# The first load becomes 32 contiguous rows, and the last diagonal tile moves into the last batch

## The chip, the cores and the metric

The kernel runs on one core of a Trainium2 chip. The metric is the device time of one execution in microseconds (us); the time given is the median of several executions. A profile is taken of one execution by the hardware, and the views below are read from it.

## What is computed

The input x has 4 batches of 4224 x 4224 numbers in fp32, 285.47 MB. The reference, cut to what matters:

```python
ps = np.cumsum(np.cumsum(x, axis=1), axis=2)   # 2D prefix sums
diag = np.diagonal(ps, axis1=1, axis2=2)       # their diagonal
return np.cumsum(diag, axis=1)                 # and its running sum
```

The output is 4 x 4224 numbers. Diagonal element i is the sum of the square x[:i+1, :i+1], so element (r, c) of x adds to every diagonal element from max(r, c) on. It is enough to know, for every m, the sum of all elements with max(r, c) = m; two running sums over m then give the output.

## The kernel before

The 4224 rows and columns are cut into 11 groups of 384 (`NG`, `GW`). Rows are loaded in strips of 768 (`F2` = 6 rows in each of 128 partitions), by DMAs issued from GpSimd (POOL) that turn fp32 into bf16 on the way; three strip buffers are in use (`NBUF`), so a load waits in POOL's queue until the strip that held its buffer has been used up. All of these loads share one queue and are served in the order in which they are issued.

For each strip `add_up` (L374) splits the elements by whether the row or the column is the larger index. Columns to the right of the diagonal block are summed down the rows by TensorE, which multiplies them with a selecting column of ones (`columns`, L363) and adds them into a tile `d` of 11 x 384 in PSUM. The diagonal block is split with a mask on VectorE (L387, L388). What lies below the diagonal is summed along the rows, partly on ScalarE (`act_sum`, L264), partly on VectorE (`row_sums`, L271). After the strips of a batch two scans on VectorE (L520) make the running sums.

The last batch ends with the last group of rows, 3840 to 4223 (`T0` = 3840, `TB` = 4096), and is ordered by hand so that little work is left after the last byte. Its rows are taken in two parts. Part a is the 256 rows from 3840 to 4095, held as `part_a` (two rows per partition, 128 apart). Part b is the last 128 rows, held as `part_b` in four blocks of `R` = 32 rows; each row of a block is spread over four partitions (`k` = 4), so a block is 128 partitions of a quarter row.

- The head (L66 to L69): before anything else, the SyncE queue (SP) loads the last 528 columns of part a in fp32, 256 pieces of 2112 bytes. It is summed by L97, its diagonal parts are masked at L322 to L325, and the result `ahead` is kept until the end.
- The tile of part b on the diagonal, 128 x 128 (`diag_b`, L427), is loaded by POOL after the first strip of the last batch and used after its second strip (L428 to L435), where all the sums that are known so far are weighed into `fin_a` and `fin_b`, the rows of the last group's outputs (`weigh_b`, `weigh_rows`, on TensorE).
- After the last whole strips POOL loads the remaining columns of part a in two cuts, 1536 to 3696 and 0 to 1536 (L472 to L474), and the four blocks of part b with their first 4096 columns (L475 to L490), the last block in two pieces of 768 and 256 columns.
- The cuts of part a are folded to 256 columns by TensorE (`fold_in`, L255, into `fold_a`) and summed by ScalarE (L539, `asum`). Block 0 is weighed by eight matmuls with `weights4_h` (L537), copied (`by`, L542) and added. Blocks 1 to 3 are summed along the rows, each partly by ScalarE and partly by VectorE (`pair_sum`, L276), and weighed into `fin_b` and `fin_e` (L550 to L578). The output rows are `yl` (first 256, then up to the last 32) and `ye` (the last 32).

The order on each engine is the order of the program (`manual_schedule`, L62), and waits between engines are set from the use of the tiles. In the tail VectorE's queue therefore holds, in this order: a pair sum of block 1, the addition L554 that needs `fin_a`, a pair sum of block 2, two of block 3, and the addition L579. ScalarE's holds the two sums of `fold_a`, the copy `by`, one sum each of blocks 1, 2 and 3, and the copy L573.

Of the kernel before, what the change touches and what calls it, by code (L numbers as in the profile page):

```python
# [8 lines left out]
FP32 = mybir.dt.float32  # L9
BF16 = mybir.dt.bfloat16  # L10
I32 = mybir.dt.int32
AX = mybir.AxisListType
# [5 lines left out]
def kernel(  # L18
# [14 lines left out]
    nc = tc.nc  # L33

    B, H, W = x.shape
    N = H
    P = 128
    F = 3
    F2 = 2 * F
    GW = P * F  # L40
    NG = N // GW
    LB = B - 1
    LG = NG - 1
    T0 = LG * GW
    TB = N - P
# [3 lines left out]
    consts = ctx.enter_context(tc.tile_pool(name="consts", bufs=1))  # L49
# [4 lines left out]
    last = ctx.enter_context(tc.tile_pool(name="last", bufs=1))  # L54
# [3 lines left out]
    psum_s = ctx.enter_context(  # L58
        tc.tile_pool(name="psum_s", bufs=1, space=bass.MemoryType.PSUM)
    )  # L60
# [2 lines left out]

    HC = 528  # L66
    src_a = x[LB, T0:TB, :].rearrange("(h p) w -> p h w", p=P)
    head = last.tile([P, 2, HC], FP32, name="head")
    nc.sync.dma_start(out=head, in_=src_a[:, :, N - HC : N])  # L69

    def strip_tile():
        return strips.tile([P, F2, N], BF16, name="strip")
# [20 lines left out]
    prefetch()  # L93


    hs = last.tile([P, 3], FP32, name="hs")
    nc.vector.reduce_sum(out=hs[:, 0:2], in_=head, axis=AX.X)  # L97

    sel = consts.tile([P, 2 * NG - 1], BF16, name="sel")
    nc.vector.memset(sel, 0.0)  # L100
# [21 lines left out]
    for i in range(1, NBUF):  # L122
        prefetch()
    um3 = upper_mask(F)
    um1 = consts.tile([P, GW], BF16, name="um1")
    nc.vector.memset(um1, 1.0)
    nc.gpsimd.affine_select(
        out=um1,
        in_=um1,
# [10 lines left out]
        out=ident,  # L140
        in_=ident,
# [10 lines left out]
    ones_row = consts.tile([NG, GW], FP32, name="ones_row")  # L152
# [21 lines left out]
    def between_groups(name, turned):  # L174
# [25 lines left out]
    weights = counted("weights", P, GW, [(0, GW, 1, 1, -1)])  # L200
    nc.gpsimd.affine_select(
        out=weights,
        in_=weights,
# [5 lines left out]
    )  # L209


    R = P // 4
    steps = consts.tile([P, P], I32, name="steps")
    nc.gpsimd.iota(steps, pattern=[[4, P]], base=7, channel_multiplier=-1)
    nc.vector.tensor_single_scalar(
        out=steps, in_=steps, scalar=2, op=ALU.arith_shift_right
    )
    weights4 = consts.tile([P, P], FP32, name="weights4")
# [5 lines left out]
    def matmul(o, lhsT, rhs, start=False):  # L224
        nc.tensor.matmul(  # L225
            o, lhsT=lhsT, rhs=rhs, start=start, stop=False, skip_group_check=True
        )
# [19 lines left out]
            )  # L247
        )

    weights4_h = consts.tile([P, P], BF16, name="weights4_h")  # L250
    nc.vector.tensor_copy(out=weights4_h, in_=weights4)
    ones_col = consts.tile([P, 1], FP32, name="ones_col")
    nc.vector.memset(ones_col, 1.0)

    def fold_in(o, src, c0, c1, w, start=False):  # L255

# [7 lines left out]
    def act_sum(acc, src):  # L264
        w = src.shape[-1]
        dump = dumpool.tile([P, 2176], BF16, name="dump")
        nc.scalar.activation(  # L267
            out=dump[:, :w], in_=src, func=ACT.Copy, accum_out=acc
        )

    def row_sums(acc, src):  # L271
        nc.vector.reduce_sum(out=acc, in_=src, axis=AX.X)  # L272
# [3 lines left out]
    def pair_sum(acc, src):  # L276

        w = src.shape[-1] // 2
        if not pairs:
            pairs.append(last.tile([P, 288], FP32, name="pair"))  # L280
        pair = pairs[0]
        nc.vector.scalar_tensor_tensor(
            out=pair[:, :w],
            in0=src[:, :w],
            scalar=1.0,
            in1=src[:, w:],
            op0=ALU.mult,
            op1=ALU.add,
            accum_out=acc,
        )  # L290

    def masked(o, i, m, acc):
        nc.vector.scalar_tensor_tensor(  # L293
            out=o,
            in0=i,
            scalar=1.0,
            in1=m,
            op0=ALU.mult,
            op1=ALU.mult,
            accum_out=acc,  # L300
        )
# [12 lines left out]
        nc.vector.memset(rows3[i], 0.0)  # L314


    ahead = last.tile([P, 2], FP32, name="ahead")
    asum = last.tile([P, 2], FP32, name="asum")
    dtot = last.tile([P, 1], FP32, name="dtot")
    hu = last.tile([P, 3], FP32, name="hu")  # L320
    hmu = last.tile([P, 3, GW], BF16, name="hmu")
    for h in range(2):  # L322
        w = GW - h * P
        masked(hmu[:, h, :w], head[:, h, HC - w : HC], um1[:, :w], hu[:, h : h + 1])
    nc.vector.tensor_sub(out=ahead, in0=hs[:, 0:2], in1=hu[:, 0:2])  # L325

    whole_sums = last.tile([NG, LB, GW], FP32, name="whole_sums")
    last_sums = last.tile([NG, GW], FP32, name="last_sums")

    M0 = 2 * P  # L330
    E0 = GW - R

    for b in range(B):
# [18 lines left out]
        def weigh_b(rows, w, r0=0, start=False):  # L352

            matmul(fin_b[:, r0:], rows, w[..., : P - r0], start=start)

        def weigh_rows(rows, start=False):

            matmul(fin_a, rows[:, 0:1], weights[:, :M0], start=start)
            matmul(fin_a[:, P:], rows[:, 1:2], weights[:, :P])
            weigh_b(rows[:, 0:1], weights[:, M0:])  # L360
            weigh_b(rows[:, 1:2], weights[:, P:])
# [55 lines left out]
        for s in range(ns):  # L417
            strip = prefetched.pop(0) if prefetched else None
            if strip is None:
                strip = strip_tile()  # L420
                load_rows(strip, b, s * F2 * P)
            add_up(
                strip, F2, s * F2 * P, acc6[:, s], um6, by_rows=whole and s > 0
            )
            if not whole and s == 0:
                diag_b = last.tile([P, P], BF16, name="diag_b")
                nc.gpsimd.dma_start(out=diag_b, in_=x[b, TB:N, TB:N])  # L427
            if not whole and s == 1:  # L428
                row_sums(hs[:, 2:3], diag_b)
                masked(hmu[:, 2, :P], diag_b, um1[:, :P], hu[:, 2:3])  # L430
                nc.vector.tensor_sub(out=dtot, in0=hs[:, 2:3], in1=hu[:, 2:3])
                for h in range(3):
                    columns(LG, h * P, GW, hmu[:, h, : GW - h * P], h > 0)
                weigh_b(dtot, weights, start=True)
                weigh_rows(ahead, start=True)  # L435
        a6 = acc6[:, :ns]
        sum_up(a6)
        for h in range(2):
            ps = slice(h * HP, (h + 1) * HP)
            k = row_of(h)  # L440
            nc.vector.tensor_copy(  # L441
                out=r6[ps, k : k + 2 * ns : 2, :], in_=a6[ps, :, :, 1]
            )

        strip = strip_tile()
# [21 lines left out]
        if not whole:  # L467

            strip = strip_tile()
            part_a = strip[:, 0:2]  # L470
            part_b = strip[:, 2, :TB].rearrange("p (s c) -> p s c", s=4)
            acuts = [(1536, N - HC), (0, 1536)]  # L472
            for c0, c1 in acuts:
                nc.gpsimd.dma_start(out=part_a[:, :, c0:c1], in_=src_a[:, :, c0:c1])  # L474
            CB = TB // 4  # L475
            bcut = 768
            for sb, c0, c1 in (
                (0, 0, CB),
                (1, 0, CB),
                (2, 0, CB),  # L480
                (3, 0, bcut),
                (3, bcut, CB),
            ):
                r0 = TB + sb * R
                nc.gpsimd.dma_start(  # L485
                    out=part_b[:, sb, c0:c1],
                    in_=x[b, r0 : r0 + R, :TB].rearrange("r (k c) -> r k c", k=4)[
                        :, :, c0:c1
                    ],
                )  # L490

            fold_a = psum_s.tile([P, 2, 256], FP32, name="fold_a")
            c0, c1 = acuts[0]
            fcuts = [c0, c0 + 768, c0 + 2048, c1]
# [13 lines left out]
        c1 = mup.tile([NG, GW], FP32, name="c1")  # L508
# [10 lines left out]
        for i, (to, src) in enumerate(((c1, d), (c2, c1))):  # L519
            nc.vector.tensor_tensor_scan(  # L520
                out=to,
# [11 lines left out]
        ye = last.tile([1, R], FP32, name="ye")  # L533
        c0, c1 = acuts[1]
        fold_in(fold_a, part_a, c0, c1, 256)
        by_ps = psum_s.tile([P, P], FP32, name="fold")
        for c in range(0, CB, P):  # L537
            matmul(by_ps, part_b[:, 0, c : c + P], weights4_h, start=c == 0)
        for h in range(2):  # L539
            act_sum(asum[:, h : h + 1], fold_a[:, h])  # L540
        by = last.tile([P, P], FP32, name="by")
        nc.scalar.copy(out=by, in_=by_ps)  # L542
        weigh_b(ones_col[0:1], last_sums[0:1, M0:])
        weigh_rows(asum)
        weigh_b(ones_col, by)


        bsum = last.tile([P, 2, 2], FP32, name="bsum")
        esum = last.tile([P, 3], FP32, name="esum")
        act_sum(bsum[:, 0, 0:1], part_b[:, 1, :512])  # L550
        pair_sum(bsum[:, 0, 1:2], part_b[:, 1, 512:])
        for i in (1, 0):
            weigh_b(bsum[:, 0, i : i + 1], weights4, R)
        nc.vector.tensor_add(out=yl[:, :M0], in0=fin_a, in1=last_sums[0:1, :M0])  # L554
# [1 line left out]
            out=out[b, T0 : T0 + M0].unsqueeze(0), in_=yl[:, :M0]  # L556
        )
        nc.sync.dma_start(
            out=out[:LB, :].rearrange("b (g i) -> g b i", i=GW), in_=whole_sums
        )  # L560
        nc.sync.dma_start(
            out=out[b, :T0].rearrange("(g i) -> g i", i=GW), in_=last_sums[1:NG]
        )
        act_sum(bsum[:, 1, 0:1], part_b[:, 2, :448])
        pair_sum(bsum[:, 1, 1:2], part_b[:, 2, 448:])
        for i in (1, 0):
            weigh_b(bsum[:, 1, i : i + 1], weights4, 2 * R)


        act_sum(esum[:, 0:1], part_b[:, 3, :320])  # L570
        pair_sum(esum[:, 1:2], part_b[:, 3, 320:bcut])
        pair_sum(esum[:, 2:3], part_b[:, 3, bcut:])
        nc.scalar.copy(out=yl[:, M0:], in_=fin_b)  # L573
        nc.sync.dma_start(
            out=out[b, T0 + M0 : T0 + E0].unsqueeze(0), in_=yl[:, M0:E0]
# [35 lines left out]
```

## Time and profile before

| | before |
|---|---|
| median of 4 executions | 667.45 us (667.18 to 667.63) |
| the profiled execution | 667.42 us |
| its span, first to last instruction | 665.7 us |
| mean granted TensorE clock | 0.656 |
| TensorE busy | 206.5 us (31%) |
| VectorE busy | 380.2 us (57%) |
| ScalarE busy | 136.9 us (21%) |
| POOL busy | 31.7 us (5%) |
| pieces that the DMA queues moved | 7666, of which under 512 bytes 698, under 2 KB another 300 |
| head, SP: size, issue to landing | 528 KB, 4.0 us |
| `diag_b`, POOL: size, issue to landing | 32 KB (as bf16), 53.2 us |

Engines are PE (TensorE matmul), PEld (its weight loads), DVE (VectorE), ACT (ScalarE), POOL (GpSimd) and SP (SyncE). "L272" is line 272 of the kernel. A row of a timeline gives the start, the duration, the engine, line and operation, what is written and read with its shape, and in brackets how long the engine had been idle before it and what ended that. The digits of a row such as DMA are the busy share in 40 equal slices of the span, in tenths. The sizes of loads that turn fp32 into bf16 are counted as they are written. A long time from issue to landing means that a transfer stood in the queue behind others.

### The profile page before, as it was taken

The page shows a single profiled execution, that of the slowest core. Times are in us where ns is not written, and L with a number is a line of the kernel's source. Part 1 is how long each engine was busy: PE and PEld are TensorE (multiplying, and loading weights), DVE is VectorE, ACT ScalarE, POOL GpSimd, SP SyncE. Part 2 cuts the span into 40 slices and gives each one's busy share as a digit, 9 for nine tenths or more (in the row PEclk, how much of TensorE's full clock was granted, in tenths as well). Part 3 has the DMA queues.
Part 4 walks back from the last instruction along what each step waited for, and adds up shares of the span by engine and source line. Part 5 has one row for each costly group of instructions (what it writes and reads, how often), then busy time and mean ns, then how long its engine had stood idle before and what let it go on. Part 6 is the DMA issues. An engine that isn't in the chain of part 4 may idle for free.

```text
span 665.7 us, 2519 instructions
## 1 busy us (share of the span) xinstructions
PE 206.5 (31%) x956; PEld 94.7 (14%) x956; DVE 380.2 (57%) x174; ACT 136.9 (21%) x223; POOL 31.7 (5%) x60
## 2 busy tenths in 40 slices
PE   0070622303117143130311623503021354350427
PEld 0030211101003021010000311201000121220203
DVE  4160928476946173756794526456589433352866
ACT  0000121406300103040630020304063002030434
POOL 4300000000000000000000000000000000001000
PEclk9995857655558585665555957567565585765759
DMA  9999999999999999999999999999999999999998
GB/s 203 218 219 219 219 218 215 212 213 218 219 218 218 219 220 217 215 216 216 213 219 220 214 218 219 219 218 214 216 215 218 218 213 219 218 219 215 216 209 165
DMA packets 7666, 143.23 MB, mean 215 GB/s; under 512 B 698, under 2 KB 998, under 8 KB 2150
## 3 DMA queue, kind: packets, MB, share of 16 engines
q0 software_dynamic: 7312, 142.47, 100.0%
q1 hardware_dynamic: 342, 0.61, 0.3%
q8 instruction: 7, 0.11, 0.1%
q14 instruction: 5, 0.04, 0.0%
HBM read 285.47 MB, written 0.07 MB: 429 GB/s over the span
## 4 chain that ended last, share of the span: by engine, by line
DVE 51%; another core or an unknown queue 35%; DMA 12%; PE 1%; issue 1%; POOL 1%; DVEq 0%; POOLq 0%
DVE acc L272 27%; DMA strip<-in_x_dram 12%; DVE mu L387 7%; DVE strip L388 7%; DVE rowed L272 7%; PE d L225 1%; DVE c L520 0%; DVE whole_sums L520 0%; POOL strip L485 0%; DVE pu L272 0%; DVE whole_sums L293 0%; POOL strip L474 0%; DVE acc L412 0%; DVE rows L441 0%
## 5 line engine op out<-in xcount | busy, mean ns | idle before, releaser
L267 ACT ACTIVATE dump<-strip 128x416 bf16<-128x416 bf16 (+6 forms) x108 | 124.3, 1151 | 519.9 <-DMA strip<-in_x_dram 517.2
L387 DVE TENSOR_TENSOR mu<-strip,um 128x4608 bf16<-128x4608 bf16 (+1 forms) x24 | 52.4, 2184 | 255.2 <-DMA strip<-in_x_dram 255.1
L272 DVE TENSOR_REDUCE acc<-strip 128x6 f32<-128x4608 bf16 (+6 forms) x23 | 195.9, 8519 | 0.4
L232 PEld LDWEIGHTS <-sel 128*11 128x11 bf16 x643 | 66.3, 103 | 472.8 <-issue 442.9
L225 PE MATMUL d<-strip,sel 128*11 128x384 bf16 x90 | 37.3, 415 | 278.2 <-DMA strip<-in_x_dram 278.2
L232 PE MATMUL d<-strip,sel 128*11 128x384 bf16 x441 | 116.2, 407 | 13.8 <-DMA strip<-in_x_dram 13.8
L388 DVE TENSOR_TENSOR strip<-strip,mu 128x4608 bf16<-128x4608 bf16 (+1 forms) x24 | 52.4, 2183 | 1.0
L225 PE MATMUL d<-mu,sel 128*11 128x384 bf16 x43 | 15.8, 366 | 108.8 <-DVE mu L387 108.8
L272 DVE TENSOR_REDUCE rowed<-strip 128x384 f32<-128x2304 bf16 x12 | 48.8, 4065 | 0.0
L232 PE MATMUL d<-mu,sel 128*11 128x384 bf16 x200 | 45.9, 364 | 0.0
L76 POOL DMA_DIRECT2D strip<-in_x_dram x23 | 15.6, 680 | 535.4 <-DVE acc L272 292.9
L267 ACT ACTIVATION_READ_ACCUMULATOR dump<-strip 128x1 f32 x108 | 20.1, 186 | 0.0
L225 PE MATMUL d<-rowed,sel_f 128*11 128x384 f32 x24 | 11.4, 564 | 21.5 <-DVE rowed L272 21.5
L225 PEld LDWEIGHTS <-sel 128*11 128x11 bf16 x134 | 13.6, 102 | 23.0 <-issue 10.5
L225 PE MATMUL d<-ident,rows 128*11 128x128 f32 x24 | 5.2, 377 | 16.8 <-DVE rows L450 16.8
L107 POOL TENSOR_SCALAR_AFFINE_SELECT um<-um 128x4608 bf16<-128x4608 bf16 (+1 forms) x2 | 5.2, 2622 | 8.8 <-DVE um L106 8.8
L106 DVE MEMSET um<- 128x4608 bf16 (+1 forms) x2 | 4.9, 2458 | 1.1 <-issue 1.1
L272 DVE TENSOR_REDUCE pu<-d 11x1 f32<-11x384 f32 x4 | 2.2, 546 | 5.6 <-PE d L225 5.6
L225 PE MATMUL d<-halves,rows 128*11 128x64 f32 x48 | 5.3, 289 | 0.0
L225 PEld LDWEIGHTS d<-rowed,sel_f 128*11 128x11 f32 x24 | 1.5, 92 | 26.4 <-DVE rowed L272 26.0
L225 PEld LDWEIGHTS d<-ident,rows 128*11 128x11 f32 x24 | 2.5, 117 | 18.9 <-DVE rows L450 11.7
L225 PEld LDWEIGHTS d<-halves,rows 128*11 128x11 f32 x48 | 4.8, 129 | 1.2 <-issue 1.1
(110 smaller groups left out, 65.2 us busy)
## 6 DMA issues: line engine op xcount, KB each, us to landing
strip<-in_x_dram POOLq DMA_DIRECT2D x18, 6336.0 KB, 72.6
strip<-in_x_dram POOLq DMA_DIRECT2D x7, 3168.0 KB, 55.8
strip<-in_x_dram POOLq DMA_DIRECT2D x1, 1080.0 KB, 49.9
strip<-in_x_dram POOLq DMA_DIRECT2D x1, 768.0 KB, 52.8
strip<-in_x_dram POOLq DMA_DIRECT2D x3, 256.0 KB, 54.1
head<-in_x_dram SPq DMA_DIRECT2D x1, 528.0 KB, 4.0
strip<-in_x_dram POOLq DMA_DIRECT2D x1, 192.0 KB, 43.2
strip<-in_x_dram POOLq DMA_DIRECT2D x1, 64.0 KB, 28.6
```

The lines of the kernel that those rows point to most:

```text
L76: nc.gpsimd.dma_start(out=o, in_=x[b, r0 : r0 + f * P, :].rearrange("(p f) w -> p f w", f=f))
L106: nc.vector.memset(um, 1.0)
L107: nc.gpsimd.affine_select(out=um, in_=um, compare_op=ALU.is_gt, fill=0.0, base=0, pattern=[[-1, f], [1, f * P]], channel_multiplier=-f,)
L225: nc.tensor.matmul(o, lhsT=lhsT, rhs=rhs, start=start, stop=False, skip_group_check=True)
L232: te.add_instruction(mybir.InstMatmult(start_tensor_calc=False, stop_tensor_calc=False, tile_position=(0, 0), tile_size=(P, P if lhsT.shap ...
L267: nc.scalar.activation(out=dump[:, :w], in_=src, func=ACT.Copy, accum_out=acc)
L272: nc.vector.reduce_sum(out=acc, in_=src, axis=AX.X)
L387: nc.vector.tensor_mul(out=mu, in0=block, in1=um)
L388: nc.vector.tensor_sub(out=block, in0=block, in1=mu)
```

## The change

The head becomes block 0 of part b: 32 contiguous rows, their first 3840 columns, as 128 partitions of 960 columns in fp32, pieces of 3840 bytes. It is still loaded by SP before anything else; one sum along the rows gives `hsum`, and its weighing with `weights4` is put beside the others after the second strip of the last batch. The tile on the diagonal becomes the whole 384 x 384 of the last group (`diag`, 384 pieces of 1536 bytes in place of 128 of 512), at the same place in POOL's queue, and what was done on the head's diagonal parts at the start is done on it after the second strip. Part a ends at column 3840 in place of 3696, the blocks of part b at 3840 in place of 4096, and block 0 is gone from the end, with its matmuls, its copy and the two tensors that they used. The shares of ScalarE and VectorE in blocks 1 to 3 are set anew for 960 columns. All bytes of x are still read once.

```diff
@@ -63,10 +63,16 @@
 
 
 
-    HC = 528
+    R = P // 4
+    CB = T0 // 4
+
+    def block(i):
+        r0 = TB + i * R
+        return x[LB, r0 : r0 + R, :T0].rearrange("r (k c) -> r k c", k=4)
+
     src_a = x[LB, T0:TB, :].rearrange("(h p) w -> p h w", p=P)
-    head = last.tile([P, 2, HC], FP32, name="head")
-    nc.sync.dma_start(out=head, in_=src_a[:, :, N - HC : N])
+    head = last.tile([P, CB], FP32, name="head")
+    nc.sync.dma_start(out=head, in_=block(0))
 
     def strip_tile():
         return strips.tile([P, F2, N], BF16, name="strip")
@@ -93,8 +99,8 @@
     prefetch()
 
 
-    hs = last.tile([P, 3], FP32, name="hs")
-    nc.vector.reduce_sum(out=hs[:, 0:2], in_=head, axis=AX.X)
+    hsum = last.tile([P, 1], FP32, name="hsum")
+    nc.vector.reduce_sum(out=hsum, in_=head, axis=AX.X)
 
     sel = consts.tile([P, 2 * NG - 1], BF16, name="sel")
     nc.vector.memset(sel, 0.0)
@@ -209,7 +215,6 @@
     )
 
 
-    R = P // 4
     steps = consts.tile([P, P], I32, name="steps")
     nc.gpsimd.iota(steps, pattern=[[4, P]], base=7, channel_multiplier=-1)
     nc.vector.tensor_single_scalar(
@@ -247,10 +252,6 @@
             )
         )
 
-    weights4_h = consts.tile([P, P], BF16, name="weights4_h")
-    nc.vector.tensor_copy(out=weights4_h, in_=weights4)
-    ones_col = consts.tile([P, 1], FP32, name="ones_col")
-    nc.vector.memset(ones_col, 1.0)
 
     def fold_in(o, src, c0, c1, w, start=False):
 
@@ -314,15 +315,11 @@
         nc.vector.memset(rows3[i], 0.0)
 
 
-    ahead = last.tile([P, 2], FP32, name="ahead")
     asum = last.tile([P, 2], FP32, name="asum")
-    dtot = last.tile([P, 1], FP32, name="dtot")
+    dsum = last.tile([P, 3], FP32, name="dsum")
+    hs = last.tile([P, 3], FP32, name="hs")
     hu = last.tile([P, 3], FP32, name="hu")
     hmu = last.tile([P, 3, GW], BF16, name="hmu")
-    for h in range(2):
-        w = GW - h * P
-        masked(hmu[:, h, :w], head[:, h, HC - w : HC], um1[:, :w], hu[:, h : h + 1])
-    nc.vector.tensor_sub(out=ahead, in0=hs[:, 0:2], in1=hu[:, 0:2])
 
     whole_sums = last.tile([NG, LB, GW], FP32, name="whole_sums")
     last_sums = last.tile([NG, GW], FP32, name="last_sums")
@@ -423,16 +420,24 @@
                 strip, F2, s * F2 * P, acc6[:, s], um6, by_rows=whole and s > 0
             )
             if not whole and s == 0:
-                diag_b = last.tile([P, P], BF16, name="diag_b")
-                nc.gpsimd.dma_start(out=diag_b, in_=x[b, TB:N, TB:N])
+                diag = last.tile([P, 3, GW], BF16, name="diag")
+                nc.gpsimd.dma_start(
+                    out=diag,
+                    in_=x[b, T0:N, T0:N].rearrange("(h p) w -> p h w", p=P),
+                )
             if not whole and s == 1:
-                row_sums(hs[:, 2:3], diag_b)
-                masked(hmu[:, 2, :P], diag_b, um1[:, :P], hu[:, 2:3])
-                nc.vector.tensor_sub(out=dtot, in0=hs[:, 2:3], in1=hu[:, 2:3])
+                row_sums(hs, diag)
+                for h in range(3):
+                    w = GW - h * P
+                    masked(
+                        hmu[:, h, :w], diag[:, h, GW - w :], um1[:, :w], hu[:, h : h + 1]
+                    )
+                nc.vector.tensor_sub(out=dsum, in0=hs, in1=hu)
                 for h in range(3):
                     columns(LG, h * P, GW, hmu[:, h, : GW - h * P], h > 0)
-                weigh_b(dtot, weights, start=True)
-                weigh_rows(ahead, start=True)
+                weigh_b(hsum, weights4, start=True)
+                weigh_b(dsum[:, 2:3], weights)
+                weigh_rows(dsum, start=True)
         a6 = acc6[:, :ns]
         sum_up(a6)
         for h in range(2):
@@ -468,25 +473,19 @@
 
             strip = strip_tile()
             part_a = strip[:, 0:2]
-            part_b = strip[:, 2, :TB].rearrange("p (s c) -> p s c", s=4)
-            acuts = [(1536, N - HC), (0, 1536)]
+            part_b = strip[:, 2, :T0].rearrange("p (s c) -> p s c", s=4)
+            acuts = [(1536, T0), (0, 1536)]
             for c0, c1 in acuts:
                 nc.gpsimd.dma_start(out=part_a[:, :, c0:c1], in_=src_a[:, :, c0:c1])
-            CB = TB // 4
-            bcut = 768
+            bcut = 704
             for sb, c0, c1 in (
-                (0, 0, CB),
                 (1, 0, CB),
                 (2, 0, CB),
                 (3, 0, bcut),
                 (3, bcut, CB),
             ):
-                r0 = TB + sb * R
                 nc.gpsimd.dma_start(
-                    out=part_b[:, sb, c0:c1],
-                    in_=x[b, r0 : r0 + R, :TB].rearrange("r (k c) -> r k c", k=4)[
-                        :, :, c0:c1
-                    ],
+                    out=part_b[:, sb, c0:c1], in_=block(sb)[:, :, c0:c1]
                 )
 
             fold_a = psum_s.tile([P, 2, 256], FP32, name="fold_a")
@@ -533,22 +532,16 @@
         ye = last.tile([1, R], FP32, name="ye")
         c0, c1 = acuts[1]
         fold_in(fold_a, part_a, c0, c1, 256)
-        by_ps = psum_s.tile([P, P], FP32, name="fold")
-        for c in range(0, CB, P):
-            matmul(by_ps, part_b[:, 0, c : c + P], weights4_h, start=c == 0)
         for h in range(2):
             act_sum(asum[:, h : h + 1], fold_a[:, h])
-        by = last.tile([P, P], FP32, name="by")
-        nc.scalar.copy(out=by, in_=by_ps)
-        weigh_b(ones_col[0:1], last_sums[0:1, M0:])
+        weigh_b(ones_row[0:1, 0:1], last_sums[0:1, M0:])
         weigh_rows(asum)
-        weigh_b(ones_col, by)
 
 
         bsum = last.tile([P, 2, 2], FP32, name="bsum")
         esum = last.tile([P, 3], FP32, name="esum")
-        act_sum(bsum[:, 0, 0:1], part_b[:, 1, :512])
-        pair_sum(bsum[:, 0, 1:2], part_b[:, 1, 512:])
+        act_sum(bsum[:, 0, 0:1], part_b[:, 1, :480])
+        pair_sum(bsum[:, 0, 1:2], part_b[:, 1, 480:])
         for i in (1, 0):
             weigh_b(bsum[:, 0, i : i + 1], weights4, R)
         nc.vector.tensor_add(out=yl[:, :M0], in0=fin_a, in1=last_sums[0:1, :M0])
@@ -561,14 +554,14 @@
         nc.sync.dma_start(
             out=out[b, :T0].rearrange("(g i) -> g i", i=GW), in_=last_sums[1:NG]
         )
-        act_sum(bsum[:, 1, 0:1], part_b[:, 2, :448])
-        pair_sum(bsum[:, 1, 1:2], part_b[:, 2, 448:])
+        act_sum(bsum[:, 1, 0:1], part_b[:, 2, :416])
+        pair_sum(bsum[:, 1, 1:2], part_b[:, 2, 416:])
         for i in (1, 0):
             weigh_b(bsum[:, 1, i : i + 1], weights4, 2 * R)
 
 
-        act_sum(esum[:, 0:1], part_b[:, 3, :320])
-        pair_sum(esum[:, 1:2], part_b[:, 3, 320:bcut])
+        act_sum(esum[:, 0:1], part_b[:, 3, :288])
+        pair_sum(esum[:, 1:2], part_b[:, 3, 288:bcut])
         pair_sum(esum[:, 2:3], part_b[:, 3, bcut:])
         nc.scalar.copy(out=yl[:, M0:], in_=fin_b)
         nc.sync.dma_start(
```

## The prediction

> **What bounds the kernel.** I read the page from the top: engine shares, slices, queues.
>
> ```profile
> PE 206.5 (31%) x956; PEld 94.7 (14%) x956; DVE 380.2 (57%) x174; ACT 136.9 (21%) x223; POOL 31.7 (5%) x60
> DMA  9999999999999999999999999999999999999998
> q0 software_dynamic: 7312, 142.47, 100.0%
> HBM read 285.47 MB, written 0.07 MB: 429 GB/s over the span
> ```
>
> No engine is near full; the DMA row is, from first slice to last. 285.47 MB is the whole of x, read once, and the change reads it once too. So the time is a start until data flow, a stream whose length is its bytes and pieces, and a tail after the last piece. Then the first operation on each strip of the last batch (timeline, VectorE; columns: start, duration, operation, idle time before it and who ended that):
>
> ```profile
> 529.00 2.56 DVE L387 TENSOR_TENSOR mu<-strip,um 128x4608 bf16<-128x4608 bf16 x1 [7.46 <-DMA strip<-in_x_dram]
> ...
> 589.09 2.56 DVE L387 TENSOR_TENSOR mu<-strip,um 128x4608 bf16<-128x4608 bf16 x1 [16.94 <-DMA strip<-in_x_dram]
> ```
>
> Each waits for its strip, so the starts are landing times. The second strip starts at 559.22: 30.22 us after the first, with `diag_b` between them; the third 29.87 us later with nothing between. A strip is 768 x 4224 x 4 = 12.976 MB, so the stream runs at 434.4 GB/s. Then the start:
>
> ```profile
> 0.82 0.45 SPq L69 DMA_DIRECT2D head<-in_x_dram  x1
> 1.33 1.22 POOL L90 DMA_DIRECT2D strip<-in_x_dram  x2 [0.81 <-POOLq L595]
> 4.84 1.25 DVE L97 TENSOR_REDUCE hs<-head 128x2 f32<-128x1056 f32 x1 [4.84 <-DMA head<-in_x_dram]
> ```
>
> The head and the first strip are launched half a microsecond apart and share the engines. Last the end (timeline):
>
> ```profile
> 657.66 0.38 PE L225 MATMUL fold_a<-strip,ident_h 128*128 128x512 bf16 x1 [0.45 <-DMA strip<-in_x_dram]
> ...
> 659.21 0.38 ACT L267 ACTIVATE dump<-fold_a 128x256 bf16<-128x256 f32 x1 [5.51 <-PE fold_a L232]
> ...
> 660.21 0.42 DVE L282 SCALAR_TENSOR_TENSOR pair<-strip 128x256 f32<-128x256 bf16 x1 [0.94 <-DMA strip<-in_x_dram]
> ...
> 660.66 0.41 DVE L554 TENSOR_TENSOR yl<-fin_a,last_sums 1x256 f32<-1x256 f32 x1
> ...
> 662.42 0.39 DVE L282 SCALAR_TENSOR_TENSOR pair<-strip 128x224 f32<-128x224 bf16 x1 [0.43 <-DMA strip<-in_x_dram]
> ...
> 662.85 0.29 DVE L282 SCALAR_TENSOR_TENSOR pair<-strip 128x128 f32<-128x128 bf16 x1
> ...
> 663.53 0.18 DVE L579 TENSOR_TENSOR ye<-fin_e,yl 1x32 f32<-1x32 f32 x1 [0.38 <-PE fin_e L225]
> ```
>
> VectorE still waits for data at 662.42; the second column cut of `part_a` (landed 657.63) is folded and summed long before, in the shadow of four more blocks. That shadow is what the change shortens.
>
> [...] `diag_b` writes 256 bytes per piece and took 0.30 us (30.22 less 29.92, the interval between first and second strip in batches 1 and 2 of the same view) where its bytes need 0.15[...]; the new pieces write 768. [...] in the rows above VectorE keeps program order.
>
> **The stream, part by part.** Bytes at 434.4 GB/s; pieces are per DMA engine (of 16).
> - Head: 540,672 bytes in 16 pieces become 491,520 in 8. By bytes 1.24 becomes 1.13, -0.11. What it really costs: the first strip landed at 35.54; less its 29.87 that is 5.67; POOL's first issue ends at 1.97, and a transfer on its own needs about 1.96 (`ye` issued 663.74, span ends 665.7); 1.74 is left for the head, 0.50 over its bytes. The gain lies between 0 (the head moves in the ramp) and 0.11 + 0.50 = 0.61. I take -0.13.
> - Diagonal tile: 65,536 bytes (0.30) become 589,824 in 24 pieces of 1536. By bytes 1.36. A 4096-byte-piece block took 1.28 (660.21 to about 661.50) against 1.21 by bytes: 0.009 per piece, so 24 add 0.21. Lower end 1.36, upper 1.36 + 24 x 0.019 = 1.81, with 0.15/8 = 0.019 from `diag_b`. I take 1.57: +1.27.
> - `part_a`: 144 more columns of 256 rows, 147,456 bytes, as many pieces: +0.34.
> - Blocks of 32 rows: now 657.63 to 662.69 (the last piece of 131,072 bytes is not shown landing; 0.30 after the one before, 662.39), 5.06. After: one block fewer, 1.28 x 960/1024 = 1.20 twice, 0.92 x 704/768 = 0.84, and 0.30: 3.54. -1.52.
>
> Sum -0.13 + 1.27 + 0.34 - 1.52 = -0.04; with the ends, -0.73 to +0.33. The last piece lands at about 662.65.
>
> **Work that is moved under cover, cost nothing.** VectorE at the second strip of the last batch: a sum over 128x3x384 (3.35 us for 3072 elements per partition on L272, so 1.26), three masked products (0.52, 0.42 from the head's, 0.28 from `diag_b`'s) and a subtraction: about 2.6 in place of 0.67. Cover: 16.9 us of idle before the next strip. POOL's next load waits for that subtraction (issue at 572.20) and slips to about 574.2; its data land some 60 us later behind two queued strips, so 45 us of backlog hide it. Uncovered, each would cost its 1.9. The bigger diag DMA adds some tenths to POOL's 0.57 us issue, with 31 us free behind it. At the start VectorE's head sum shrinks (960 elements for 1056), the early masks and two weights set-ups go; nothing waits for them. TensorE loses eight 128-wide matmuls (0.61), ScalarE the `by` copy (0.26): both lay in the tail's shadow. The block DMA that goes takes its POOL issue and its wait for a landing with it, 28 us ahead of need.
>
> **The tail, on the path.** After the second `part_a` cut came 5.06 us of blocks; now 3.54. So it lands at 662.65 - 3.54 = 659.11, 1.48 later. In queue order:
> - TensorE: six fold matmuls, `fold_a` done at 660.6. Behind them wait all weighing matmuls.
> - ScalarE: the two `asum` sums start at 660.69 and 661.20 (period 0.51 as at 659.21, 659.72). Then 480, 416 and 288 wide sums, 0.60, 0.55, 0.44 by the line through 0.63/512, 0.58/448, 0.47/320, each plus 0.13 for its accumulator read: the last result, `esum` 0, at 663.65, against 662.97 before: +0.68.
> - VectorE: the `yl` add needs `fin_a`, thus `asum`: 660.66 + 1.48 = 662.14. Three pair sums queue behind it, though their data are there: 0.41, 0.44, 0.38 plus 0.04 each put the last pair at 663.49, against 662.85: +0.64.
> - Both feed `fin_e`, then `ye`: 663.53 + 0.64 = 664.17; the `yl` copy on ScalarE (about 663.8) is in time. SP's three earlier output DMAs slip from 661.1 to 662.6 and are issued by 663.7, before `ye` at 664.4.
>
> So 0.64 is the whole change (it contains the stream's -0.04). By the ends: the stream's -0.73 to +0.33 moves all of this one for one; 0.25 either way for the tail's own steps.
>
> **The sum.** The profiled execution took 667.42, 1.72 around its span of 665.7, and is 0.03 under the median 667.45. 667.42 + 0.64 = 668.06; as a median 668.1.
>
> **Rivals.**
> - *The start pays*: the new head[...] saves the full 0.61. Stream -0.52, time 667.6. For it: the unexplained 0.50. Against: ramp and head can't be told apart here.
> - *The tail absorbs it*: the last piece still sets the end, as it does now: 667.45 - 0.04 = 667.4. For it: VectorE's idle 0.94 at 660.21 and 0.43 at 662.42 before its pairs, which I count as used up. Against: ScalarE comes out late by itself, from durations that the trace shows.
> - *Small pieces hurt* (slower): the diag tile moves at `diag_b`'s rate, 65,536 bytes in 0.30 us, 218 GB/s: 2.71 in place of 1.57. 668.1 + 1.14 = 669.2, +0.27%. It passes 0.2% once the tile needs over 2.27 us, under 260 GB/s. For it: the only diagonal piece measured. Against: its pieces were three times smaller.
> - The change does what it says: the pieces and widths follow from the shapes.
>
> **Chances.** Forecast 0.66 (667.4 to 668.7), start pays 0.14, absorbed 0.08, small pieces 0.12. 0.2% is 1.33 us, about what a measurement of this kernel can tell from no change. Slower by more: most of small pieces (0.10) and the top of the forecast (0.09), 0.19. Faster by more would need the start to give over 1.9 us, more than the 1.74 that the head can hold: 0.02. Same: 0.79. Range 667.2 to 669.0: it takes in the two lower rivals and leaves out small pieces and the edges.
>
> **What would show it.** Right: the second strip of the last batch about 1.2 us later after the first than now, the last `part_b` pair without idle before it, the `yl` add ending just before a chain of three pair sums, the chain of waits ending through `asum` and `yl` rather than a DMA. Wrong: a diag interval over 32 us (small pieces), a first strip at 35.0 or earlier (the start pays), or a last pair that still waits for DMA.

## The result and the profile after

| | before | changed |
|---|---|---|
| median | 667.41 us (52 executions) | 668.43 us (34 executions) |
| lowest to highest | 667.08 to 668.97 | 668.13 to 669.01 |
| the profiled execution | 667.42 us | 668.29 us |
| its span | 665.7 us | 666.6 us |

The ratio is 1.0014, with a 95% interval of 1.0009 to 1.0019: the changed kernel is 0.6 to 1.3 us slower. The forecast was 668.1, that is 0.64 more; the measured shift of the medians is 1.02.

The page of the changed kernel, the same lines as before:

```profile
PE 206.7 (31%) x948; PEld 93.7 (14%) x948; DVE 380.7 (57%) x171; ACT 136.7 (21%) x222; POOL 31.4 (5%) x59
DMA  8999999999999999999999999999999999999998
q0 software_dynamic: 7424, 142.49, 99.8%
HBM read 285.47 MB, written 0.07 MB: 428 GB/s over the span
```

The DMA row is still full in all but the first and the last slice and no other engine is near full, so the difference must lie in the stream's length or in what follows it. The landings of the last batch's strips (timeline, VectorE):

```profile
529.19 2.56 DVE L384 TENSOR_TENSOR mu<-strip,um 128x4608 bf16<-128x4608 bf16 x1 [7.45 <-DMA strip<-in_x_dram]
...
560.69 2.56 DVE L384 TENSOR_TENSOR mu<-strip,um 128x4608 bf16<-128x4608 bf16 x1 [21.36 <-DMA strip<-in_x_dram]
...
590.61 2.56 DVE L384 TENSOR_TENSOR mu<-strip,um 128x4608 bf16<-128x4608 bf16 x1 [15.10 <-DMA strip<-in_x_dram]
```

The first lands 0.19 later than in the profile before. The interval to the second is 31.50 where it was 30.22: that is the 384-wide diagonal tile. The next, 29.92, has nothing in it. At the start (timeline):

```profile
0.82 0.61 SPq L75 DMA_DIRECT2D head<-in_x_dram  x1
1.32 1.22 POOL L96 DMA_DIRECT2D strip<-in_x_dram  x2 [0.81 <-POOLq L588]
4.72 1.15 DVE L103 TENSOR_REDUCE hsum<-head 128x1 f32<-128x960 f32 x1 [4.72 <-DMA head<-in_x_dram]
```

The head lands hardly sooner (4.72 for 4.84) with 9% fewer bytes, and SP takes longer to issue it (0.61 for 0.45). The end (timeline):

```profile
659.50 0.38 PE L230 MATMUL fold_a<-strip,ident_h 128*128 128x512 bf16 x1 [0.20 <-DMA strip<-in_x_dram]
...
661.06 0.38 ACT L268 ACTIVATE dump<-fold_a 128x256 bf16<-128x256 f32 x1 [5.84 <-PE fold_a L237]
...
662.51 0.41 DVE L547 TENSOR_TENSOR yl<-fin_a,last_sums 1x256 f32<-1x256 f32 x1 [0.95 <-PE fin_a L230]
...
663.31 0.38 DVE L283 SCALAR_TENSOR_TENSOR pair<-strip 128x208 f32<-128x208 bf16 x1
...
663.73 0.29 DVE L283 SCALAR_TENSOR_TENSOR pair<-strip 128x128 f32<-128x128 bf16 x1
...
664.44 0.18 DVE L572 TENSOR_TENSOR ye<-fin_e,yl 1x32 f32<-1x32 f32 x1 [0.41 <-PE fin_e L230]
```

VectorE now waits for `fin_a` before the `yl` add, and its last pair sums have no idle time before them: their data are there already. The chain of waits says the same. Before, it went from a DMA straight to the last pair sums. Now it runs through the fold and ScalarE's queue (columns: start, length, what):

```profile
659.88 1.09 PE fold_a L237 x5
...
661.06 0.48 ACT dump L268 x2
...
663.25 0.20 ACT dump L268
...
663.47 0.44 ACT dump L268
...
664.06 0.29 PE fin_e L230 x4
```

The account of the two profiles, from the starts above: the second cut of part a is folded 1.84 us later (659.50 for 657.66), of which 0.19 came before the last batch, 1.28 is the tile, 0.33 the longer first cut and 0.04 the rest. From there to `ye` it now takes 4.94 us where it took 5.87, so 0.93 is given back. 1.84 - 0.93 = 0.91, the shift of `ye`. The blocks alone would have given back about 1.5, by the forecast's durations.

### The profile page after: what moved, and what is told of

The parts are those of the page before. It is cut to its first block, busy times and chain, and to the rows that moved or that the text cites. A ratio compares the mean times of both kernels' runs of the same rounds, so it can differ in the third digit from the quotient of the medians.

```text
span 666.6 us, 2498 instructions
## 1 busy us (share of the span) xinstructions
PE 206.7 (31%) x948; PEld 93.7 (14%) x948; DVE 380.7 (57%) x171; ACT 136.7 (21%) x222; POOL 31.4 (5%) x59
## 3 DMA queue, kind: packets, MB, share of 16 engines
q0 software_dynamic: 7424, 142.49, 99.8%
## 4 chain that ended last, share of the span: by engine, by line
DVE 53%; another core or an unknown queue 34%; DMA 8%; PE 3%; issue 1%; POOL 1%; ACT 0%; DVEq 0%; ACTq 0%
DVE acc L273 28%; DMA strip<-in_x_dram 7%; DVE mu L384 7%; DVE strip L385 7%; DVE rowed L273 7%; PE d L230 1%; POOL um L113 1%; DVE um L112 1%; DMA head<-in_x_dram 1%; DVE c L519 0%; DVE whole_sums L519 0%; PE fold L237 0%; PE fold_a L237 0%; DVE pu L273 0%
## 5 line engine op out<-in xcount | busy, mean ns | idle before, releaser
L268 ACT ACTIVATE dump<-strip 128x416 bf16<-128x416 bf16 (+5 forms) x108 | 124.3, 1151 | 520.8 <-DMA strip<-in_x_dram 518.0
```

Of the source, the lines that this page charges most:

```text
L268: nc.scalar.activation(out=dump[:, :w], in_=src, func=ACT.Copy, accum_out=acc)
```

## The experiments

The theory: the stream is nearly as long as before, and the loss lies in the tail, where the chain of work that starts from the last cut of part a has lost the block that covered it, that is, the load during which it could run unseen. The rival: a later stream is the whole loss, and the queues behind the cut cost nothing. Two more questions came up on the way: what the head costs, and what TensorE's clock does.

### The cover put back

```diff
 for sb, c0, c1 in (
+    (0, 0, CB),
     (1, 0, CB),
```

> The changed kernel with block 0 of part b loaded once more between part a and block 1, and not used: 480 KB more, at the place that block 0 had in the kernel before. Its DMA needs 1.20 us. Tail theory: the shadow over the asum chain is back, so 1.2 of stream costs only about 0.6, 669.05, and ScalarE and VectorE wait for blocks again. Stream theory: the full 1.2, 669.6.

Measured: 668.88 us (14 executions), ratio 1.0021 (1.0013 to 1.0029). 1.2 us more of stream cost about 0.5, by the medians 668.88 - 668.43. The first sums of blocks 1, 2 and 3 in this kernel (timeline, VectorE and ScalarE):

```profile
662.12 0.41 DVE L283 SCALAR_TENSOR_TENSOR pair<-strip 128x240 f32<-128x240 bf16 x1 [0.52 <-DMA strip<-in_x_dram]
...
663.33 0.55 ACT L268 ACTIVATE dump<-strip 128x416 bf16<-128x416 bf16 x1 [0.33 <-DMA strip<-in_x_dram]
...
664.20 0.38 DVE L283 SCALAR_TENSOR_TENSOR pair<-strip 128x208 f32<-128x208 bf16 x1 [0.41 <-DMA strip<-in_x_dram]
```

Each of them waits for its block again, as in the kernel before, and the chain of waits runs from a DMA straight to the last pair sums, as it did there. The stream theory's 1.2 is out.

### The cover taken away from the kernel before

```diff
-(0, 0, CB),
...
-    matmul(by_ps, part_b[:, 0, c : c + P], weights4_h, start=c == 0)
...
-nc.scalar.copy(out=by, in_=by_ps)
...
-weigh_b(ones_col, by)
```

> The kernel before without the load of block 0 in the tail and without the matmuls and the copy that use it: 512 KB less, its part of the output's last group is left out. The stream ends 1.28 us sooner. Tail theory: the last cut of part a still lands at 657.6, the chain behind it (4.97 us from landing to ye in the changed kernel) puts ye at about 662.65 in place of 663.53, so only 0.85 to 0.95 is gained: 666.5. Stream theory: 1.28 gained, 666.1.

Measured: 666.84 us (21 executions), ratio 0.9997 (0.9989 to 1.0005). Neither theory: the gain is smaller than both. The trace shows why. The first cut of part a landed at about 653.7 (the last half strip's 648.65 plus the 5.09 that its bytes need), but TensorE was still at earlier work (timeline):

```profile
653.13 0.85 PE L232 MATMUL d<-mu,sel 128*11 128x384 bf16 x2
653.77 1.14 PE L225 MATMUL d<-halves,rows 128*11 128x64 f32 x12
654.84 0.39 PE L225 MATMUL fold_a<-strip,ident_h 128*128 128x512 bf16 x1
```

It was slow because of its clock: these rows of two and of twelve matmuls took 0.85 and 1.14 us, the same rows of the kernel before 0.49 and 0.83. Busy time by stage, first of this kernel, then of the kernel before (columns: stretch, length, then busy time and count of TensorE, its weight loads, VectorE, ScalarE, POOL, then the granted TensorE clock, DMA share, GB/s):

```profile
651.00:652.00 1.00, 1.00 (x4) 0.20 (x3) 1.00 (x1) 0.97 (x3) 0.00 (x0) 0.50 1.10 225
...
654.00:655.00 1.00, 1.00 (x13) 0.84 (x12) 0.32 (x2) 0.00 (x0) 0.00 (x0) 0.80 1.13 224
```

```profile
651.00:652.00 1.00, 1.00 (x5) 0.25 (x3) 1.00 (x1) 1.00 (x2) 0.00 (x0) 0.76 1.02 207
652.00:653.00 1.00, 1.00 (x10) 0.62 (x8) 1.00 (x1) 0.97 (x2) 0.00 (x0) 1.00 1.06 213
```

Both begin this burst of matmuls at 648.6 to 648.9 after 10.7 us of idle time. The kernel before had the full clock 2.6 us later (651.49), this one only after 5.8 (654.39). In the changed kernel it took 4.5 (650.38 to 654.84; the expectations further down have 654.67 and, for this run, 654.2). In the twelve profiles of this case in which TensorE was not warmed up the delay runs from 2.6 to 5.8 us; what sets it is not shown. Under the old cover a late clock had 0.4 to 0.9 us of idle time (VectorE's, before its pair sums) to be lost in. Without it, this one reaches the end.

### The short tail with the clock up

36 matmuls without use are put on TensorE ahead of the last half strip:

```diff
+for _ in range(36):
+    matmul(fold_g, ident_h, um6[:, 0:3, 0:160], start=True)
 wp, ws = 1280, 1280 + 1536
```

> The kernel before without block 0 in its tail (its part of the output's last group is left out), as in the run of the short tail, with the same 36 matmuls ahead. In the short tail the first cut of part a landed at about 653.7 and was folded only from 654.84, with the clock granted in full from 654.2. Clock theory: the fold starts at 653.7 to 653.9 again, and 0.4 to 0.8 of the missing gain comes back: 666.3, with a narrow spread. Rival (the missing gain lies elsewhere): 666.8.

Measured: 666.48 us (22 executions), ratio 0.9986 (0.9979 to 0.9992). TensorE's granted clock was 1.00 from 649 to 656, and it waits for the cut again (timeline):

```profile
654.12 0.38 PE L225 MATMUL fold_a<-strip,ident_h 128*128 128x512 bf16 x1 [1.60 <-DMA strip<-in_x_dram]
```

The fold starts at 654.12 and not by 653.9, since this stream was 0.2 later. The gain is the one that the tail theory gave for the short tail without a late clock: 0.9 of the 1.28 us of stream. So, by medians, about 0.35 us is what the lost cover costs in this form, and the late clock cost another 0.36 on top (666.84 to 666.48). The two intervals touch, so these sizes are rough. The profiles agree on the clock: from the last whole strip of the batch to `ye` this kernel takes 43.88 us (618.95 to 662.83), the short tail with the late clock 44.53 (618.73 to 663.26). The narrow spread that was expected did not come (666.23 to 669.28), though executions over 668 became fewer, 1 of 22 where there were 6 of 21.

### The changed kernel with the clock up

The same edit on the changed kernel.

> The changed kernel with 36 matmuls of 480 columns without use on TensorE ahead of the last half strip, so that its clock is full when that strip lands (it was granted in full only from 654.67 in the changed kernel, 651.49 in the kernel before). Clock theory (the tail behind part a is now exposed, so TensorE's late clock costs time there): the first cut of part a is folded as it lands at 655.8, 0.15 to 0.3 us sooner, time 668.2 and the executions lie closer together. Rival (the clock plays no part, cut and queues alone): 668.4 with the same spread.

Measured: 668.40 us (21 executions), ratio 1.0016 (1.0010 to 1.0022), and the spread grew: 14 executions at 668.07 to 668.77, 7 at 669.27 to 669.84. The profile is one of the seven (timeline, then the stage):

```profile
655.76 0.38 PE L230 MATMUL fold_a<-strip,ident_h 128*128 128x512 bf16 x1 [1.96 <-DMA strip<-in_x_dram]
...
657.95 1.91 PE L237 MATMUL fold_a<-strip,ident_h 128*128 128x512 bf16 x4
```

```profile
656.00:657.00 1.00, 1.00 (x8) 0.48 (x7) 0.11 (x1) 0.00 (x0) 0.00 (x0) 0.95 1.05 209
657.00:658.00 1.00, 1.00 (x6) 0.31 (x4) 0.34 (x1) 0.00 (x0) 0.00 (x0) 0.50 1.06 207
```

With the clock up early (1.00 from 643.5) TensorE was done early, sat idle for 1.96 us, and lost the clock in the middle of the tail (at 656.91); four folds took 1.91 us in place of 1.03, and `ye` began at 665.42, 0.98 later than in the changed kernel. The expectation's gain of 0.15 to 0.3 is not there: in the changed kernel the clock came at 654.84 and the cut was folded at 655.97, close to its landing at about 655.8. That the clock can reach the end of this tail is shown, in the other direction. Other profiles say from when on. Five profiles of kernels with the changed kernel's tail have the full clock 3.0 to 4.5 us after the burst began, and take 43.98 to 44.00 us from the last whole strip to `ye`, whatever their head or diagonal tile. A sixth, with another head (below), has it after 5.4, and takes 44.38. So in the profile of the changed kernel the clock cost nothing. Whether the other six long executions of this run lost the clock as well is not shown; the run with a head of 128 rows (below) has six from 669.42 up without any warm-up.

### Opening the tail

First with one edit, the second cut in two pieces:

```diff
-acuts = [(1536, T0), (0, 1536)]
+acuts = [(1536, T0), (512, 1536), (0, 512)]
```

> The changed kernel with the second column cut of part a loaded in two pieces, 512 to 1536 and 0 to 512, each folded as it lands. Tail theory (the end is set by the chain from the last cut of part a through its fold, asum, and the queues of ScalarE and VectorE behind it): only two fold matmuls are left after the last cut, so asum starts about 0.85 us sooner, the pair sums wait for their data again, and ye starts about 0.6 sooner, at 663.85 in place of 664.44; time 667.85. Stream theory (the whole 0.95 us is a later stream, the queues cost nothing): one DMA more, no gain, 668.4 to 668.5.

Measured: 668.27 us (13 executions), ratio 1.0009 (1.0001 to 1.0017), `ye` at 664.51. The expected 0.6 is a miss: `asum` started only 0.20 sooner and something else held its result up. The clock was late as well, 5.0 us after the burst began (timeline):

```profile
661.46 0.37 PE L230 MATMUL fin_b<-last_sums,ones_row 1*1 1x128 f32 x2 [0.70 <-DVE last_sums L519]
661.76 0.81 PE L230 MATMUL fin_a<-weights,asum 128*1 128x256 f32 x4
```

A second chain runs beside the first: last half strip, first cut's fold, the matmuls on `r3`, the two scans, `last_sums`. Its weighing stands ahead of `asum`'s in TensorE's queue. Both are opened by three edits more:

```diff
+for q in range(F):
+    matmul(d[:, q : GW : F], r3[:, :, q], ident)
 fold_part(0)
-for q in range(F):
-    matmul(d[:, q : GW : F], r3[:, :, q], ident)
...
-weigh_b(ones_row[0:1, 0:1], last_sums[0:1, M0:])
 weigh_rows(asum)
+weigh_b(ones_row[0:1, 0:1], last_sums[0:1, M0:])
...
+pair_sum(bsum[:, 1, 1:2], part_b[:, 2, 416:])
 nc.vector.tensor_add(out=yl[:, :M0], in0=fin_a, in1=last_sums[0:1, :M0])
```

> The changed kernel with three edits of the tail: the second cut of part a in two pieces; the matmuls on r3 ahead of the first fold of part a and the weighing of last_sums behind that of asum on TensorE; the yl add behind the pair sum of block 2 on VectorE. Tail theory with two chains (through asum, and through the scans to last_sums; the run with three cuts opened only the first): both are open, the last pair sum waits for its block, ye at about 663.9 in place of 664.44, time 667.85 to 667.95. Stream theory: 668.4.

Measured: 668.08 us (13 executions), ratio 1.0004 (0.9996 to 1.0012); the profiled execution took 667.85, 0.44 less than the changed kernel's. `ye` began at 663.91, as expected (timeline):

```profile
661.75 0.44 DVE L283 SCALAR_TENSOR_TENSOR pair<-strip 128x272 f32<-128x272 bf16 x1 [0.36 <-DMA strip<-in_x_dram]
...
662.61 0.37 DVE L283 SCALAR_TENSOR_TENSOR pair<-strip 128x208 f32<-128x208 bf16 x1
...
663.91 0.18 DVE L572 TENSOR_TENSOR ye<-fin_e,yl 1x32 f32<-1x32 f32 x1 [0.59 <-PE fin_e L230]
```

The pair sum of block 2 waits for its data again; the last two don't, though the last one was expected to, and the chain of waits still runs through the fold and ScalarE. The medians give 0.35 for these four edits, and the two intervals overlap. In the profile half of the gain of 0.53 in `ye` is not theirs: its last whole strip landed 0.27 sooner than the changed kernel's (620.19 for 620.46), and from there to `ye` it took 43.72 us for 43.98, so 0.26 belongs to the edits. The place is shown by the trace, the size only roughly, and not all of the tail's loss was taken back. No form of the changed kernel was faster than the kernel before.

### Piece size of the diagonal tile

```diff
-in_=x[b, T0:N, T0:N].rearrange("(h p) w -> p h w", p=P),
+in_=x[b, T0 : T0 + P, 0 : 3 * GW].rearrange("p (h w) -> p h w", h=3),
```

> The changed kernel with the diagonal tile read from one contiguous stretch of each of 128 rows (pieces of 4608 bytes, as many bytes in all; the last group's output is then not that of the diagonal). In the changed kernel the first to second strip of the last batch took 31.50, of which 1.58 is the tile, 1.36 by its bytes. Piece theory (0.009 us a piece): 31.35 and 0.15 less time, 668.3. Rival (pieces cost nothing, the rest is the DMA's own): 31.50, 668.4. Second rival (small pieces are the loss): under 31.2, 668.0.

Measured: 668.31 us (13 executions), ratio 1.0011 (1.0002 to 1.0019). The queue moved 256 pieces fewer (7168 for 7424) and the interval was 31.43 (529.18 to 560.61) in place of 31.50. Sixteen pieces fewer per engine (256 over 16) saved 0.07 us, 0.004 a piece, midway between the two theories. It may be scatter: the other profiles with the 1536-byte pieces have 31.38 to 31.50 for this interval. So the prediction's 0.009 a piece is not confirmed, and small pieces as the loss, under 31.2, are out. The tile costs its bytes, 1.36, and 0.1 to 0.2 besides, which `diag_b` with its 0.30 for 0.15 of bytes cost as well.

### The head

```diff
-nc.sync.dma_start(out=head, in_=block(0))
+nc.sync.dma_start(out=head, in_=src_a[:, :, 3696:4176])
...
```

> The changed kernel with a head of as many bytes but in the old shape: 256 pieces of 1920 bytes [...] from rows of part a; its sum goes where that of block 0 went, so the last group's output lacks block 0. Start theory (the head's pieces set when the first strip lands, and this is lost again by the third strip): the first strip lands at about 35.5 in place of 34.85, the third at 95.5 as in both kernels, time 668.4, within 0.2 of the changed kernel. Rival (the start pays to the end): the whole stream is 0.6 to 0.8 later, 669.1.

Measured: 668.08 us (22 executions), ratio 1.0011 (1.0004 to 1.0017). The first strip landed at 35.02, neither theory's number, and the stream was 0.30 to 0.37 sooner in the last batch. So a head of half as large pieces is not the slower one. In this profile the lead was lost again: `ye` began at 664.48, 0.04 later than in the changed kernel. This is the profile whose clock came 5.4 us after the burst began. Next, 128 rows in place of 32:

```diff
+nc.sync.dma_start(out=head, in_=x[LB, TB:N, :CB])
```

> The changed kernel with the head read from 128 rows, 960 columns of each (the last 128 rows, their first 960 columns), in place of 32 rows in four pieces each: as many bytes, the same 128 pieces of 3840 bytes; the last group's output then lacks block 0. The first strip of the last batch landed at 528.98 to 529.22 in six profiles with the 32-row head and at 528.77 to 529.00 in four with heads of 256 pieces, and the run with such a head of equal bytes was 0.35 faster. Row theory (the four-fold split of 32 rows is slow): 528.9 here too, 668.1. Piece theory (8 pieces per engine against 16): 529.1, 668.4. Scatter: neither, anything between.

Measured: 668.27 us (22 executions), ratio 1.0014 (1.0007 to 1.0021). Its stream was as early, and `ye` began at 664.05. And no head:

```diff
-nc.sync.dma_start(out=head, in_=block(0))
+nc.vector.memset(head, 0.0)
```

> The changed kernel without the load of the head (its tile is set to zero on VectorE; the last group's output lacks block 0): 480 KB less at the start. If the head's bytes count in full beside the first strip: everything 1.13 us sooner, 667.3. If it moves in the time before the first strip's data flow: no gain, 668.4. By the 1.74 us that the prediction left for the old head, up to 1.6.

Measured: 667.90 us (13 executions), ratio 1.0004 (0.9996 to 1.0012). Both kernels were profiled once more, for the scatter:

> The kernel before once more, for the scatter of a profile: the first strip lands anywhere between 34.5 and 35.7, the first strip of the last batch at 528.8 to 529.1, and the time at which TensorE's clock is granted in full in the tail moves [...] with no effect on the end, 667.4.

> The changed kernel once more, for the scatter of a profile: the first strip lands anywhere between 34.5 and 35.7, the first strip of the last batch at 529.0 to 529.3; a late clock puts ye later, an early one sooner, within 668.1 to 669.0.

Measured: 667.83 and 668.30 us. The kernel before fell outside what was expected, the changed kernel inside it. Landings in the profiles (us):

| head | first strip | third strip | first strip of the third batch | first strip of the last batch |
|---|---|---|---|---|
| none | 34.45 | 94.90 | 364.30 | 528.82 |
| 128 rows, 128 pieces, 480 KB | 35.71 | 95.45 | 364.47 | 528.85 |
| 256 rows, 256 pieces, 480 KB | 35.02 | 95.21 | 364.48 | 528.89 |
| 256 rows, 256 pieces, 528 KB (before) | 35.64 | 95.47 | 364.61 | 529.00 |
| the same, before again | 36.30 | 96.03 | 365.06 | 529.43 |
| the same, the two short tails | 34.55, 35.35 | 95.37, 95.59 | 364.38, 364.60 | 528.77, 529.00 |
| 32 rows, 128 pieces, 480 KB (changed) | 34.85 | 95.51 | 364.60 | 529.19 |
| the same, changed again | 34.92 | 95.49 | 364.62 | 529.24 |
| the same, five other kernels | 34.63 to 34.90 | 95.25 to 95.65 | 364.61 to 364.85 | 528.98 to 529.22 |

By the last batch all heads but the 32-row one stand where no head stands, within 0.2 us, but for one profile of the kernel before that was late from its first strip and stayed 0.4 late. The 32-row head stands 0.2 to 0.4 later than no head in seven profiles, and its issue on SP took 0.61 us where that of 128 rows took 0.40. Yet the changed kernel and the kernel before are level as late as 364.6; the 0.19 between them appears in the next 30 us (394.73 for 394.56), long after the head has landed. So these profiles don't show that the head causes it, and against the other profile of the kernel before the changed one is 0.2 earlier. The executions lean against the 32-row head without settling it: 12 of 22 with 256 rows, and 8 of 22 with 128, were faster than the fastest of the changed kernel's 34 (668.13), but 2 and 6 of them were slower than its slowest (669.01), and for the 128-row head the medians differ by 0.16 only.

So: more than half of the head's time is hidden, shown by the run without one, which gained 0.5 us and not 1.13; that the split of 32 rows costs about 0.3 is possible, and not shown.

A lead at the first strip does not last. The 32-row head's is 0.8 against the kernel before and nothing at the third; without a head the lead is 1.2, then 0.6, and 0.2 in the last batch. Four profiles with the old head have their first strip anywhere from 34.55 to 36.30. Why the leads fade stays open.

## Why the prediction was right

The sign held, and so did the main step: the tail gives back less than the stream loses, because VectorE and ScalarE now come out late behind the last cut of part a. The size held roughly: +0.64 was forecast, 0.6 to 1.3 measured, 0.87 between the two profiles, 1.02 between the medians, so the forecast lies at the low end. Several terms were off.

- **Diagonal tile.** +1.27 forecast, +1.28 measured. That the value is so close is partly luck: I priced 24 pieces at 0.009 each, where the run with long pieces shows 0.004, itself within the scatter; the rest of what the tile costs over its bytes did not change with the pieces.
- **Part a.** +0.34 forecast, +0.33 measured.
- **Blocks.** Forecast -1.52 for the stream. The padded kernel shows block 1 to block 2 in 1.21 us (662.12 to 663.33) and block 2 to the last one's first piece in 0.87 (to 664.20); I had 1.20 and 0.84.
- **Head.** -0.13 forecast; between the two profiles the stream is 0.19 later ahead of the last batch. This is the largest error, 0.32, and whether the head makes it is open, as said above. What failed is the reading of the first strip's landing as the head's price. Without any head the first strip lands 1.19 sooner than in the profile before, which looks like the full 1.24 of the head's bytes; but only 0.18 of it is left in the last batch, and the same head in four profiles scatters by 1.75 at the first strip. For the same reason a first strip at 35.0 or earlier, which I had named as a sign that the start pays, was a bad sign: it came (34.85), and the start did not pay.
- **Tail.** The cut lands 1.84 later in place of 1.48: 0.32 is the head's term, 0.04 other. From there the forecast had 5.06 us from landing to `ye` and the trace 4.97 (landing at about 659.47). The chain of waits goes through `asum` and ScalarE's sums behind it, not through `yl`; but ScalarE's last read ends at 664.01 and VectorE's at 664.03, so the two are level, about as I had them. The step that I did not name is the second chain, through `last_sums`: it was level too, which the run with three cuts showed.
- **Work under cover.** VectorE's work at the second strip took 2.6 us (572.94 to 575.51), as forecast, and the strips after it landed on time, so nothing was paid. POOL's next load did not wait for the subtraction, as I had said it would; it went out before that began at 575.35 (timeline; by the profile it waited for the row sums of the strip), so that my 574.2 is close is luck.

```profile
573.67 1.10 POOL L82 DMA_DIRECT2D strip<-in_x_dram  x2 [33.09 <-DVE acc L273]
```

- **Rivals.** "The start pays" is out: whatever the head gave at the first strip was gone by the third (95.51 for 95.47). "The tail absorbs it" is out by the pair sums without idle time and by the padded kernel. "Small pieces hurt" is out: the interval is 31.50, not over 32.

In sum, between the two profiles, about 0.3 of the shift of 0.91 in `ye` is the stream (0.19 ahead of the last batch, 1.28 for the tile, 0.33 for part a, 0.04 other, less about 1.5 for the blocks) and about 0.6 the tail, of which the four edits of the tail took back roughly half.

## What to carry to other kernels

Where a stream of loads sets the time, a load that comes late in it covers the chain that starts from the load before it, so that moving it away may free less than its bytes (here 1.2 us of stream were worth about 0.5). Before such a load is moved to the front, follow every queue behind the last few loads to the end, in program order, and look for the second chain that is level with the first. Ask also what the cover hid that was no work at all; here it hid when TensorE's clock came up (without the cover, 666.84 us in the short tail as it was and 666.48 with the clock up early).

## What the runs showed of the hardware

- TensorE's clock came back 2.6 to 5.8 us after a burst began, in twelve profiles of kernels that differ little. In the changed kernel's tail a delay of up to 4.5 cost nothing (43.98 to 44.00 us from the last whole strip to `ye` in five profiles), one of 5.4 came with 0.40 more. In one profile it was lost again in a tail, 1.15 us after work had resumed from 1.96 us of idle time; `ye` then began about 1 us later. Keeping TensorE busy ahead of the tail went with a lower median in one kernel (666.84 to 666.48), and with two groups of executions in another (14 at 668.07 to 668.77, 7 at 669.27 to 669.84).
- Of the 1.13 us that the bytes of a 480 KB load need, issued by SP half a microsecond ahead of a long stream from POOL, about 0.5 was left at the end (668.43 with it, 667.90 without). The lead of the kernel without it was 1.2 us at the first strip against the kernel before and 0.2 by the last batch.
- When the first strip landed said little about when the later ones did: the kernel before had it at 35.64 and 36.30 in two profiles, with two shortened forms at 34.55 and 35.35, and 0.8 us of difference to the changed kernel was gone two strips later.
- A DMA inside a full queue cost an estimated 0.1 to 0.2 us beside its bytes, at 8 pieces of 512 bytes per engine (0.30 for 0.15) and at 8 of 4608 (1.51 for 1.36) alike. With 24 pieces of 1536 bytes it was 0.07 more, which is within the scatter of that interval.
